# Pacing the up projections of the latent heads between attention steps

## The chip, the cores and the metric

The kernel runs on one core of a Trainium2 chip. The metric is the device time of one execution in microseconds (us). Engines are named as in the profile: PE is TensorE's matmul, PEld its weight load, DVE is VectorE, ACT is ScalarE, POOL is GpSimd, SP is SyncE, which issues the DMAs.

## The reference

One layer of a hybrid encoder, 1024 tokens of width 1024, batch 1, all in float32:

```
mod = silu(c) @ w_ada + b_ada          # 6 rows: shift, scale, gate, twice
h   = rmsnorm(x) * (1 + sc_a) + sh_a
q_lat(256), kv_lat(128), k_rope(32), ca_qkv(3*512) = split(h @ w_in)
q   = rmsnorm(q_lat) @ w_q_up          # 8 heads of 96 = 64 + 32 rotary
kv  = rmsnorm(kv_lat) @ w_kv_up        # 8 heads of 64 (key) + 64 (value)
k   = concat(k_nope, k_rope for every head)
q, k = rope(rmsnorm(q)), rope(rmsnorm(k))
o_mla = softmax(q k^T, chunk-causal, chunks of 64) v
o_ca  = softmax(cq ck^T + rel_bias, band of 9 chunks) cv     # 8 heads of 64
x = x + g_a * (concat(o_mla, o_ca) @ w_out)
h = rmsnorm(x) * (1 + sc_m) + sh_m
gate, val = split(causal_dwconv(h @ w_up, width 3))
x = x + g_m * ((silu(gate) * val) @ w_down)
```

## The kernel before

Every float32 product is made of three matmuls of split operands (high by high, high by low, low by high): `gemm3` writes them, lines 153 to 155 in the profile. The tokens are cut into 8 tiles of 128. The program has three parts: a start (normalising, the first q and k columns), an attention part (from about 86 to 706 us of the profile), and the output projection with the MLP.

**Units of attention.** The attention part goes through 32 units: a head and one half (512) of the queries. First come 16 of chunk attention, named here c, pair, head of the pair, half: c00_0, c00_1, c01_0 up to c31_1. Then 16 of latent attention: m, group of four heads, head, half: m00_0 to m13_1. A unit has scores for its row maxima (`guard`), a step that turns the maxima into a row (`mrow`), and for each block of 128 keys a step of transposed scores with exponentials (`st`) and a step of values (`val`). A unit's blocks are interleaved with the preparation of the unit two ahead (`prep`: turning q and k) and the guards of the unit one ahead. The last `val` of a unit normalises the output and stores it to DRAM (line 846, from tile `ric` for chunk heads and `rim` for latent ones).

**Fillers.** Between attention steps stand pieces of the projections that later units need. They are Python generators in a fixed list: `v0`, `qk1`, `qk2`, `v1`, `qk3` (columns of chunk heads), `m` (the latents: `f_m`), `up0`, `up1` (up projections of the two groups of latent heads), `oca` (the output projection's part over the chunk heads, stored as partial sums). Each `next` on a generator lays a few matmuls of one PSUM tile, with the eviction and the work behind it when the tile is complete, and yields a cost in nanoseconds by a formula of matmul columns alone:

```
yield 3 * len(part) * max(107, w / 2.4 + 2.5)
```

An up projection has two such steps for each token tile: `qu` (six matmuls of 384 columns), whose output is copied (`uqr`, line 616), squared, summed, rooted on POOL (line 119), scaled and rotated on POOL (lines 530 to 533); and `ku` (three matmuls of 512 columns), whose output is copied (`kraw`, line 632), split into values (lines 455 and 457), squared, summed, rooted on POOL and scaled (lines 639 to 644). Its cost counts none of the work after the matmuls.

**The pacing.** `pace` adds the attention step's cost (again from matmul columns) times a ratio to a debt, and lays fillers until their yielded costs have paid it. The ratio is `R_CA` in chunk units and `R_MLA` in latent units. When a unit's preparation needs a filler that is not done, `need` lays the rest of it at once: the latent units need `up0` or `up1`. `fill_step` also calls a side generator, `f_ada`, once for every 2000 of filler cost of `qk1` to `m` (not of `v0`, `up0`, `up1`, `oca`); it loads conditioning weights (`aw`, line 489) and sums them on DVE (`aacc`, lines 491 and 493).

**What sets the order.** The program order so made is a priority. The scheduler of the language then places instructions on each engine's queue, attention steps with a higher priority (`OFF_S`, `OFF_V`), and a filler's matmuls no earlier than an attention matmul four places back (`LAG`). [...]

Of the kernel before, what the change touches and what calls it, by code (L numbers as in the profile page):

```python
# [40 lines left out]
TB = 1  # L41
HI_ON, HL_BUFS = "pa", 3
VSCALE = 2.0 ** 14
R_CA, R_MLA = 1.17, 0.42


C_C, C_GA, C_GM, C_B, C_GQL, C_GKL = 0, 8, 16, 24, 72, 74
# [14 lines left out]
def layer_kernel(ctx, tc, I, out):  # L62
# [9 lines left out]
    def hi_of(eng, o, i):  # L72
        if eng == "a":
            act.activation(o, i, AF.Copy)  # L74
        elif eng == "p":
            pool.tensor_scalar(o, i, 1.0, 0.0, op0=MUL, op1=ADD)  # L76
        else:
            dve.tensor_copy(o, i)

    def lo_of(eng, o, i, hi):  # L80
        (pool if eng == "p" else dve).tensor_tensor(o, i, f32(hi), op=SUB)  # L81
# [34 lines left out]
    def rsqrt_mean(r, ss, n, cols=None):  # L116
        sc = ss if cols is None else ss[:, cols]
        pool.tensor_scalar(sc, sc, 1.0 / n, EPS, op0=MUL, op1=ADD)
        pool.tensor_tensor(r, ss, nhalf[:].to_broadcast(list(r.shape)), op=ALU.pow)
# [17 lines left out]
    def rtile(name, shape=(P, 512), dt=F32):  # L137
        return apg.tile(list(shape), dt, name=name, tag="R", bufs=4)

    def qtile(name):  # L140
        return apg.tile([P, 512], F32, name=name, tag="sq", bufs=2)
# [19 lines left out]
    def gemm3_f(pt, pairs, step=GSTEP):  # L161
        n, w = len(pairs), pt.shape[-1]
        for i0 in range(0, n, step):
            part = pairs[i0:i0 + step]
            if len(trail) > LAG:
                with tc.issue_after(trail[-1 - LAG]):
                    gemm3(pt, part, i0 == 0, i0 + step >= n)
            else:
                gemm3(pt, part, i0 == 0, i0 + step >= n)
            yield 3 * len(part) * max(107, w / 2.4 + 2.5)  # L170
# [218 lines left out]
    def pow2_scale(nm, ssw, b2, n, fac):  # L389
        t = cst.tile([P, 3, ND], F32, name=f"vs{nm}")  # L390
        dve.tensor_tensor(t[:, 0, :n], ssw, b2, op=MUL)
        pt = ps.tile([P, 512], F32, name=f"vsp{nm}", tag="mm", bufs=2)
        pe.matmul(pt[:, :n], ones[:], t[:, 0, :n], start=True, stop=True)
        dve.tensor_reduce(t[:, 1, 0:1], pt[:, :n], axis=AX.X, op=ADD)
        dve.tensor_scalar(t[:, 1, 0:1], t[:, 1, 0:1], fac, 1e-30, op0=MUL, op1=ADD)
        pool.tensor_tensor(t[:, 1, 1:2], t[:, 1, 0:1], nhalf[:], op=ALU.pow)
        ab = cst.tile([P, 2], F32, name=f"vab{nm}")
        dve.tensor_scalar(t[:, 2, 0:1].bitcast(I32), t[:, 1, 1:2].bitcast(I32), 0x7F800000, None, op0=ALU.bitwise_and)
        dve.reciprocal(t[:, 2, 1:2], t[:, 2, 0:1])
        dve.tensor_scalar(t[:, 2, 1:2], t[:, 2, 1:2], 1.0001, None, op0=MUL)  # L400
        dve.tensor_scalar(t[:, 2, 1:2].bitcast(I32), t[:, 2, 1:2].bitcast(I32), 0x7F800000, None, op0=ALU.bitwise_and)
        dve.tensor_scalar(ab[:, 0:1], t[:, 2, 0:1], VSCALE, None, op0=MUL)
        dve.tensor_scalar(ab[:, 1:2], t[:, 2, 1:2], 1.0 / VSCALE, None, op0=MUL)
        return ab[:, 0:1], ab[:, 1:2]
# [42 lines left out]
    def v_tile(pl, name, tag, bufs):  # L447
        v = pl.tile([P, 4, 2, 3, 64], F16, name=name, tag=tag, bufs=bufs)
        pool.memset(v[:, :, 0, 1], 1.0)
        pool.memset(v[:, :, 1, 1], 0.0)  # L450
        return v
# [120 lines left out]
    def g4(shape, dt, name):  # L572
        return G["4"].tile(shape, dt, name=name, tag="G4", bufs=8)

    def g3(shape, dt, name):
        return G["3"].tile(shape, dt, name=name, tag="G3", bufs=16)

    mq, mk, mv = {}, {}, {}

    def f_up(gr):  # L580
        if gr == 0:
            right.__exit__(None, None, None)
            for i in "4v3":
                G["cm" + i] = tc.tile_pool(name="gp" + i, bufs=1, side="right", reuse_waits="tile")
                G[i] = G["cm" + i].__enter__()
        wq = []
        for k in range(2):
            raw = qtile(f"wqr{gr}_{k}")
            sp.dma_start(raw[:, :384], I["w_qu"][gr][:, k, :])
            w = g4([P, 2, 512], F32R, f"wq{gr}_{k}")  # L590
            hi_of("a", w[:, 0, :384], raw[:, :384])
            lo_of("p", w[:, 1, :384], raw[:, :384], w[:, 0, :384])
            wq.append(w)
        raw = qtile(f"wkr{gr}")
        sp.dma_start(raw[:], I["w_kvu"][gr])
        ssw = cst.tile([P, 1], F32, name=f"sswm{gr}")
        junk = qtile(f"wkj{gr}")
        act.activation(junk[:, 0:256].rearrange("p (a b) -> p a b", a=4),
                       raw[:].rearrange("p (a b) -> p a b", a=4)[:, :, NOPE:], AF.Square, accum_out=ssw[:])
        vscale["m", gr] = pow2_scale(f"m{gr}", ssw[:], gb2[:], 1, float(KVR))  # L600
        sc = vscale["m", gr][0]
        wk = g4([P, 2, 512], F32R, f"wk{gr}")
        hi_of("a", wk[:, 0], raw[:])
        lo_of("p", wk[:, 1], raw[:], wk[:, 0])
        for t in range(NT):
            h, j = divmod(t, 4)
            sl = slice(j * P, (j + 1) * P)
            if t % 2 == 0:
                mq[gr, t // 2] = g3([P, 2, 4, QK], F32, f"qn{gr}_{t}")
                mk[gr, t // 2] = g3([P, 2, 4, QK], F32, f"kn{gr}_{t}")  # L610
                mv[gr, t // 2] = v_tile(G["v"], f"vt{gr}_{t}", "Gv", 8)
            pt = ps.tile([P, 512], F32, name=f"qu{gr}_{t}", tag="mm", bufs=2)
            yield from gemm3_f(pt[:, :384], [(latT[k, h][:, 0, sl], latT[k, h][:, 1, sl], wq[k][:, 0, :384], wq[k][:, 1, :384])
                                for k in range(2)])
            raw = rtile(f"uqr{gr}_{t}")
            act.activation(raw[:, :384], pt[:, :384], AF.Copy)
            sq = qtile(f"usq{gr}_{t}")
            act.activation(sq[:, :384], raw[:, :384], AF.Square)
            ss = cst.tile([P, 4], F32, name=f"uss{gr}_{t}", tag="ss", bufs=4)
            r = cst.tile([P, 4], F32, name=f"ur{gr}_{t}", tag="rr", bufs=4)  # L620
            dve.tensor_reduce(ss[:], sq[:, :384].rearrange("p (a b) -> p a b", a=4), axis=AX.X, op=ADD)
            rsqrt_mean(r[:], ss[:], QK)
            q_t = mq[gr, t // 2][:, t % 2]
            dve.tensor_tensor(q_t, raw[:, :384].rearrange("p (a b) -> p a b", a=4),
                              r[:].unsqueeze(2).to_broadcast([P, 4, QK]), op=MUL)
            rope_apply(q_t[:, :, NOPE:], q_t[:, :, NOPE:], tabq, t, 4, raw[:, 0:256])
            pt = ps.tile([P, 512], F32, name=f"ku{gr}_{t}", tag="mm", bufs=2)
            yield from gemm3_f(pt[:], [(latT[2, h][:, 0, sl], latT[2, h][:, 1, sl], wk[:, 0], wk[:, 1])])
            p4 = pt[:].rearrange("p (a b) -> p a b", a=4)
            raw = rtile(f"kraw{gr}_{t}")  # L630
            r3 = raw[:, :256].rearrange("p (a b) -> p a b", a=4)
            act.activation(r3, p4[:, :, 0:NOPE], AF.Copy)
            v_set(mv[gr, t // 2], slice(2 * (t % 2), 2 * (t % 2) + 2),
                  p4[:, :, NOPE:].rearrange("p (c o) b -> p c o b", c=2), sc)
            s3 = raw[:, 256:512].rearrange("p (a b) -> p a b", a=4)
            act.activation(s3, r3, AF.Square)
            ss = cst.tile([P, 4], F32, name=f"kss{gr}_{t}", tag="ss", bufs=4)
            r = cst.tile([P, 4], F32, name=f"kr{gr}_{t}", tag="rr", bufs=4)
            dve.tensor_reduce(ss[:], s3, axis=AX.X, op=ADD)
            pool.tensor_tensor(ss[:], ss[:], ssr[:, t:t + 1].to_broadcast([P, 4]), op=ADD)  # L640
            rsqrt_mean(r[:], ss[:], QK)
            k_t = mk[gr, t // 2][:, t % 2]
            dve.tensor_tensor(k_t[:, :, 0:NOPE], r3, r[:].unsqueeze(2).to_broadcast([P, 4, NOPE]), op=MUL)
            pool.tensor_tensor(k_t[:, :, NOPE:], kr[:, t:t + 1, :].to_broadcast([P, 4, ROPE]),
                               r[:].unsqueeze(2).to_broadcast([P, 4, ROPE]), op=MUL)


    def load_wo(k0, n, he, le):
        ws = []
# [436 lines left out]
    def mt(tag, shape, name, dt=F32):  # L1086
        return mp.tile(list(shape), dt, name=name, tag=tag, bufs=MB[tag])
# [85 lines left out]
    for h in range(2):  # L1173
# [4 lines left out]
        for j in range(NF):  # L1178
# [4 lines left out]
            gr = mt("s", [P, 512], f"gr{h}_{j}")  # L1183
# [10 lines left out]
        for t in range(4):  # L1194
            xt = mt("u", [P, D], f"xo{h}{t}")
            sp.dma_start(xt[:], x1_d[4 * h + t])
            for n in range(2):
                c = slice(n * 512, (n + 1) * 512)
# [78 lines left out]
```

## Time and profile before

| | us |
|---|---|
| median of 3 runs | 1513.79 (1511.94 to 1515.04) |
| the profiled execution | 1509.98 |
| its span in the profile, first to last instruction | 1508.2 |
| PE busy in the span | 1326.6 (88%) |
| DVE busy | 1017.8 (67%) |
| POOL busy | 828.9 (55%) |
| ACT busy | 713.8 (47%) |
| granted clock of TensorE, mean | 0.941 |

Views of the profile are named in words: the page has the share of each engine in 40 slices, in tenths; the table by stage gives each engine's busy time in stretches that one chooses; groups are instructions of one line, engine and operation, with count, busy time and mean duration; waits say which line waited for which; the stores at line 846 tell when each unit of attention ended.

### The profile page before, as it was taken

What the parts mean: (1) busy time and instruction counts of PE and PEld (TensorE: products, weight loads), DVE (VectorE), ACT (ScalarE), POOL (GpSimd) and SP (SyncE); (2) the same over time, 40 slices, a digit from 0 to 9 for tenths busy, and PEclk for the clock granted to TensorE, in tenths of its full rate; (3) what the DMA queues carried; (4) which work ended last, traced back from release to release, by engine and by line L of the source; (5) the groups of instructions that cost most, each with busy time, mean ns of one, the idle gap of its engine ahead of it and who ended that gap; (6) DMA issues with size and microseconds to landing.
All of it is one profiled execution on the core that took longest, in us unless ns stands there. A gap on an engine that the chain in (4) does not pass through costs nothing.

```text
span 1508.2 us, 19999 instructions
## 1 busy us (share of the span) xinstructions
PE 1326.6 (88%) x6926; PEld 1057.8 (70%) x6926; DVE 1017.8 (67%) x1421; ACT 713.8 (47%) x1319; POOL 828.9 (55%) x901
## 2 busy tenths in 40 slices
PE   3769999899878899988927859999999999999997
PEld 2668878778645566655816648888888887887885
DVE  8926676656467756674676668888777788666653
ACT  5435566466446667674354324444444433333331
POOL 5764443363599834222867246666556564665663
PEclk9979999999768899998958979999999999999999
DMA  8321223321110232124621142222222235446442
GB/s 309 122 67 43 71 60 94 93 74 46 57 28 12 65 94 91 58 76 144 216 98 56 56 154 84 84 84 84 72 82 84 85 120 174 146 143 239 156 141 98
DMA packets 80002, 153.02 MB, mean 101 GB/s; under 512 B 8215, under 2 KB 44315, under 8 KB 79901
## 3 DMA queue, kind: packets, MB, share of 16 engines
q1 hardware_dynamic: 79900, 151.75, 30.4%
q8 instruction: 54, 0.88, 0.2%
q14 instruction: 48, 0.39, 0.1%
HBM read 122.88 MB, written 28.84 MB: 101 GB/s over the span
## 4 chain that ended last, share of the span: by engine, by line
PE 49%; DVE 17%; DMA 14%; POOL 10%; issue 6%; ACT 4%; SPq 0%; DVEq 0%; ACTq 0%; POOLq 0%
DMA aw<-w_ada 7%; PE p L1121 5%; PE p L1119 5%; PE p L1120 5%; PE dnp L1193 4%; PE dnp L1191 4%; PE dnp L1192 4%; DMA wu<-w_up 2%; PE tm L810 2%; DVE aacc L493 2%; DVE u L1127 2%; DVE adaw L368 1%; DVE u L1128 1%; PE tc L810 1%; DVE wu L1149 1%
## 5 line engine op out<-in xcount | busy, mean ns | idle before, releaser
L81 POOL TENSOR_TENSOR wds<-wd,wds 128x512 fp32r<-128x512 f32 x88 | 154.2, 1771 | 99.3 <-ACT wds L74 99.2
L74 ACT ACTIVATE wds<-wd 128x512 fp32r<-128x512 f32 x88 | 54.6, 624 | 151.9 <-PE dnp L1193 149.9
L1191 PE MATMUL dnp<-wds,g 128*128 128x512 f32 x308 | 119.6, 390 | 3.8 <-DVE c L1153 1.9
L1193 PE MATMUL dnp<-wds,g 128*128 128x512 f32 x308 | 118.3, 389 | 1.6 <-DVE g L81 1.6
L1192 PE MATMUL dnp<-wds,g 128*128 128x512 f32 x308 | 119.7, 389 | 0.0
L1181 DVE TENSOR_TENSOR wd<-wd,gmbc 128x1024 f32<-128x1024 f32 x44 | 68.0, 1544 | 73.7 <-DMA wd<-w_down 73.7
L81 POOL TENSOR_TENSOR wa<-wu,wa 128x512 fp32r<-128x512 f32 x22 | 38.5, 1749 | 90.7 <-ACT wa L74 90.7
L81 POOL TENSOR_TENSOR wc<-ws,wc 128x512 fp32r<-128x512 f32 x22 | 51.8, 2353 | 65.9 <-ACT wc L74 65.9
L493 DVE SCALAR_TENSOR_TENSOR aacc<-aw,cs,aacc 128x256 f32<-128x256 f32 x84 | 43.4, 517 | 64.5 <-DMA aw<-w_ada 64.0
L821 DVE TENSOR_TENSOR hlm<-pm,hlm 128x512 f16<-128x512 f32 (+2 forms) x96 | 57.6, 608 | 38.4 <-POOL hlm L76 19.6
L81 DVE TENSOR_TENSOR g<-gr,g 128x512 fp32r<-128x512 f32 x44 | 71.0, 1615 | 12.3 <-ACT g L74 12.1
L814 ACT ACTIVATE pc<-tc,sca 128x512 f32<-128x512 f32 (+3 forms) x96 | 50.1, 525 | 60.0 <-DVE hlc L821 45.0
L1127 DVE SCALAR_TENSOR_TENSOR u<-c,pk,u 128x1023 f32<-128x1023 f32 x44 | 75.6, 1726 | 4.1 <-ACT u L1126 4.1
L810 PE MATMUL tm<-qt,kt 96*128 96x512 f16 (+7 forms) x288 | 71.3, 339 | 4.8 <-ACT hlm L818 1.8
L810 PEld LDWEIGHTS <-kt 128*128 128x128 f16 (+2 forms) x480 | 46.1, 101 | 36.5 <-issue 18.4
L1191 PEld LDWEIGHTS dnp<-wds,g 128*128 128x128 f32 x308 | 57.8, 188 | 17.0 <-DVE xo L1199 2.7
L76 POOL TENSOR_SCALAR hlm<-pm 128x384 f16<-128x384 f32 (+2 forms) x48 | 25.7, 535 | 79.4 <-ACT pm L814 50.5
L1126 ACT ACTIVATE u<-c,pk 128x1024 f32<-128x1024 f32 x44 | 52.3, 1236 | 33.8 <-DVE c L1159 33.8
L1193 PEld LDWEIGHTS dnp<-wds,g 128*128 128x128 f32 x308 | 57.8, 188 | 14.2 <-DVE g L81 2.0
L821 DVE TENSOR_TENSOR hlc<-pc,hlc 128x512 f16<-128x512 f32 (+3 forms) x96 | 54.8, 578 | 17.5 <-POOL hlc L76 10.0
L1192 PEld LDWEIGHTS dnp<-wds,g 128*128 128x128 f32 x308 | 57.8, 188 | 11.7
L1128 DVE SCALAR_TENSOR_TENSOR u<-c,pk,u 128x1022 f32<-128x1022 f32 x44 | 65.8, 1530 | 0.0
(432 smaller groups left out, 4714.7 us busy)
## 6 DMA issues: line engine op xcount, KB each, us to landing
wu<-w_up SPq DMA_DIRECT2D x44, 512.0 KB, 3.7
wd<-w_down SPq DMA_DIRECT2D x44, 512.0 KB, 3.5
aw<-w_ada SPq DMA_DIRECT2D x96, 128.0 KB, 2.1
g_d<-u SPq DMA_DIRECT2D x22, 512.0 KB, 2.6
gr<-g_d SPq DMA_DIRECT2D x44, 256.0 KB, 3.1
x<-x SPq DMA_DIRECT2D x16, 512.0 KB, 7.6
adaw<-w_ada_a SPq DMA_DIRECT2D x16, 512.0 KB, 5.0
wq_r<-w_qk SPq DMA_DIRECT2D x32, 128.0 KB, 2.7
```

Of the source, the lines that this page charges most:

```text
L81: (pool if eng == "p" else dve).tensor_tensor(o, i, f32(hi), op=SUB)
L493: dve.scalar_tensor_tensor(acc[:], w[:], cs[:, k:k + 1], acc[:], op0=MUL, op1=ADD)
L810: last = pe.matmul(s[:, c0:c1], l, m, start=(y == 0), stop=(y == len(todo) - 1))
L821: dve.tensor_tensor(hl[:, 1, :w], p[:, :w], hl[:, 0, :w], op=SUB)
L1119: pe.matmul(pt, sh, pg[:, 0], start=(k == 0), stop=False)
L1120: pe.matmul(pt, sh, pg[:, 1], start=False, stop=False)
L1121: pe.matmul(pt, sl, pg[:, 0], start=False, stop=(k == 3))
L1127: dve.scalar_tensor_tensor(u[:, 1:], c[:, :S - 1], pk[:, cv + 1:cv + 2], u[:, 1:], op0=MUL, op1=ADD)
L1128: dve.scalar_tensor_tensor(u[:, 2:], c[:, :S - 2], pk[:, cv:cv + 1], u[:, 2:], op0=MUL, op1=ADD)
L1191: pe.matmul(pts[t][n], sh, w[n][:, 0], start=(j == 0), stop=False)
L1192: pe.matmul(pts[t][n], sh, w[n][:, 1], start=False, stop=False)
L1193: pe.matmul(pts[t][n], sl, w[n][:, 0], start=False, stop=(j == NF - 1))
```

## The change

The generator `f_up` is renamed `f_up_steps`, and a new `f_up` passes its steps on with their costs multiplied by `UP_W` = 4.0. `R_CA` goes from 1.17 to 1.42 and `R_MLA` from 0.42 to 0.64. The list of fillers, their instructions and their tiles are the same; which fillers lie after which attention step is not.

```
-R_CA, R_MLA = 1.17, 0.42
+R_CA, R_MLA = 1.42, 0.64
+UP_W = 4.0
...
-    def f_up(gr):
+    def f_up_steps(gr):
         if gr == 0:
             right.__exit__(None, None, None)
...
+    def f_up(gr):
+        for c in f_up_steps(gr):
+            yield c * UP_W
+
     def load_wo(k0, n, he, le):
```

## The prediction

> **What bounds the kernel now.** I read the page first, for where TensorE is not full. Its slices are 37.7 us each.
>
> ```profile
> span 1508.2 us, 19999 instructions
> PE   3769999899878899988927859999999999999997
> POOL 5764443363599834222867246666556564665663
> PEclk9979999999768899998958979999999999999999
> ```
>
> Counted from slice 0, PE falls to 8, 7, 8, 8 in slices 10 to 13 (377 to 528 us) and is back at 9 after them. In the same four slices POOL stands at 5, 9, 9, 8 and the granted clock at 7, 6, 8, 8. So the kernel has one sick stretch inside its attention part. The other one, slice 20, is the turn to the MLP, which the change does not touch.
>
> Next, the times at which a unit's output is stored (start, duration, queue, line), one row for each unit of attention; they put the stretch into the program. I use these eight; chunk attention writes through `ric`, latent attention through `rim`.
>
> ```profile
> 199.51 0.45 SPq L846 DMA_DIRECT2D oT_d<-ric  x1
> ...
> 235.36 0.45 SPq L846 DMA_DIRECT2D oT_d<-ric  x1
> ...
> 404.71 0.45 SPq L846 DMA_DIRECT2D oT_d<-ric  x1
> 415.64 0.45 SPq L846 DMA_DIRECT2D oT_d<-ric  x1
> 469.65 0.45 SPq L846 DMA_DIRECT2D oT_d<-ric  x1
> ...
> 529.46 0.45 SPq L846 DMA_DIRECT2D oT_d<-rim  x1
> ...
> 666.02 26.64 SPq L846 DMA_DIRECT2D oT_d<-rim  x4
> 706.23 0.45 SPq L846 DMA_DIRECT2D oT_d<-rim  x1
> ```
>
> In order they are the ends of units c01_1, c10_1, c30_1, c31_0, c31_1, m01_0, m11_1 (the first of its four) and m13_1, the last. The table by stage, cut at these ends (us, then busy of PE, PEld, DVE, ACT, POOL with instruction counts, clock, DMA share, GB/s):
>
> ```profile
> 369.00:404.70 35.70, 32.10 (x174) 26.85 (x173) 14.27 (x30) 16.57 (x52) 22.46 (x61) 0.83 0.17 52
> 404.70:529.50 124.80, 99.77 (x443) 67.12 (x443) 85.80 (x198) 71.63 (x157) 102.51 (x189) 0.79 0.13 40
> 415.60:469.60 54.00, 40.57 (x159) 27.11 (x157) 35.35 (x87) 28.67 (x67) 49.31 (x101) 0.72 0.08 22
> 469.60:489.60 20.00, 16.09 (x78) 11.47 (x79) 16.00 (x38) 12.42 (x29) 19.09 (x36) 0.83 0.04 8
> 529.50:666.00 136.50, 126.57 (x728) 82.87 (x727) 86.93 (x167) 97.31 (x178) 43.73 (x50) 1.00 0.26 83
> 666.00:706.20 40.20, 33.26 (x174) 18.03 (x173) 24.11 (x46) 24.67 (x44) 5.56 (x12) 0.88 0.18 52
> ```
>
> From 415.6 to 469.6 POOL is busy 49.31 of 54.0 us (91%) and PE 40.57 (75%) at clock 0.72; from 529.5 to 666 PE is busy 126.57 of 136.5 us (93%) at clock 1.00. What POOL does there, by groups (count | busy, mean ns of one | idle before), and who waits in 400 to 520 us (us in all, times, longest):
>
> ```profile
> L119 POOL TENSOR_TENSOR ur<-uss,nhalf 128x4 f32<-128x4 f32 x16 | 17.5, 1091 | 0.2
> L119 POOL TENSOR_TENSOR kr<-kss,nhalf 128x4 f32<-128x4 f32 x15 | 15.7, 1045 | 0.7
> ACT uqr L616 <- DVE kn L643: 8.6, 4, 2.8
> PE ku L153 <- DVE vt L457: 5.6, 4, 3.0
> ```
>
> These are steps of the up projections: two roots of about 1.05 us for every token tile, hardly any idle time in front of them. TensorE waits at `ku` because the evicting engines are behind. When the sixteen tiles began and ended, and TensorE's part of one tile:
>
> ```profile
> 408.17 0.67 PE L153 MATMUL qu<-wq,latT 128*128 128x384 f32 x1
> 472.87 0.42 PE L153 MATMUL qu<-wq,latT 128*128 128x384 f32 x1
> ...
> 474.47 0.39 PE L155 MATMUL ku<-wk,latT 128*128 128x512 f32 x1
> 515.33 1.01 POOL L119 TENSOR_TENSOR kr<-kss,nhalf 128x4 f32<-128x4 f32 x1
> ```
>
> Sixteen tiles take 515.33 + 1.01 - 408.17 = 108.2 us, 6.8 us each. TensorE needs for one tile's nine matmuls from 472.87 to the last start at 474.47 and one more pitch, about 1.8 us. The lump is paced by POOL and by the chain through it, not by TensorE.
>
> **What the change moves.** No instruction is added or taken away; the order in which fillers are laid between attention steps changes, and the two head groups' tiles with it. By the code's own costs a tile of the up projections counts 975 + 647.5 = 1622.5; now it counts 6490. A pair of chunk units counts 16,404, a pair of latent units 17,870. Before: 16,404 x 1.17 / 1622.5 = 11.8 tiles in a chunk pair. After: 16,404 x 1.42 / 6490 = 3.6, and in a latent pair 17,870 x 0.64 / 6490 = 1.8. Stepping through the pacing with these costs gives: before, `m` ends in c30_0 and all 16 tiles follow in c30_0 to c31_1; the output partials (`oca`, 32 steps) run from m00_0 to m11_1. After, `m` ends in c21_0; 12 tiles come in c21_0 to c31_1 (two of them forced at the preparation of m00_0, which needs the first group), 4 in m00_0 to m02_0, and the 32 steps from m02_1 to m12_0.
>
> **Prices.** (1) A chunk pair: c10 took 235.36 - 199.51 = 35.85 us with 30 filler steps of six matmuls. Their pitch is shown by eleven matmuls in a row, of which the first and the last are:
>
> ```profile
> 205.78 0.28 PE L154 MATMUL ipq<-wq_s,hT 128*128 128x256 f32 x1
> ...
> 206.97 0.28 PE L155 MATMUL ipq<-wq_s,hT 128*128 128x256 f32 x1
> ```
>
> 1.19 us over ten pitches, 0.714 us a step; 35.85 - 21.4 = 14.4 us for 16,404 units of cost, 0.88 us per thousand. (2) A latent unit: 666.0 to 706.2 holds m12 and m13 without fillers, 32,959 of cost in 40.2 us, 1.22 us per thousand. All latent units, 140,019, are 170.8 us. (3) A step of the partials: of 64 matmuls of each kind 529.5 to 666 shows
>
> ```profile
> L154 PE MATMUL oc<-wo,ch 128*128 128x512 f32 x55 | 22.9, 417 | 0.0
> ```
>
> 55, so 27.5 of 32 steps; the units there (m01_1 to m11_1, 82,614) cost 100.8 us, and (136.5 - 100.8) / 27.5 = 1.30 us a step, 41.6 us in all. Partials thus cost the same wherever they lie, and packing them denser is booked at nothing: PE covers them at 93% in that window; were that cover gone, the 7% idle there on 41.6 us is 3 us.
>
> **The sum.** The end of `m` moves ahead of c21_1 and c30: 26,237 x 0.88 = 23.1 us. It also loses its drain. In 369.0 to 404.7 TensorE does 32.10 x 0.83 = 26.6 us of work at full clock, so 9.1 us are lost while the last tiles of `m` are normalised, turned round and followed at once by the up projections, with nothing else to lay between. After the change chunk attention from c21_1 to c31_1 is there to lay between. `m` ends at 404.7 - 23.1 - 9.1 = 372.5 us.
>
> From there to the end of c31_1: by PE alone 42,201 x 0.88 + 12 x 1.8 = 58.7 us; at the lump's pitch 12 x 6.8 = 81.6 us. I take the second: 3.6 tiles a pair is still denser than POOL's 91% row permits at 14.4 us a pair. End: 454.1 (431.2 by the other). Units m00_0 to m02_0: 42,316 x 1.22 + 4 x 1.8 = 58.8 us, POOL far from full; 512.9 (490.0). The rest: 170.8 - 51.6 + 41.6 = 160.8 us; 673.7 (650.8). Before it was 706.2. The gain is 32.5 us (55.4), and what follows, the output projection and the MLP, is unchanged. The profiled execution took 1509.98 us, 3.8 under the median of 1513.79; so 1477.5 there, 1481 for the median (1458 by the other end).
>
> The denser first part: 16,404 x 1.42 in place of x 1.17 lays 35.6 for 29.3 steps of 655 into a chunk pair. That only brings TensorE work forward. Its one other queue is the conditioning's: one filler cost of 2000 calls the next part of it, so those transfers come closer together. Their issues go through SP and their sums through DVE, which waits for them from 86 to 400 us:
>
> ```profile
> DVE aacc L493 <- DMA aw<-w_ada: 59.0, 49, 3.2
> ```
>
> 59.0 us over 49 waits, 1.2 us each, with all attention's DVE work queued behind. PE was full there all the same (c10 above), so I book nothing; if the cover fails, a fifth more waits in the same time is 59.0 x 0.21 = 12 us. A gain there has no ground, as nothing is left out.
>
> **A rule that speaks against it.** In the rows above clock follows feeding: 1.00 at 93% busy, 0.88 at 83% (666 to 706), 0.72 at 75%. [...] What lower rates would make of the time is worked out in the first two rivals.
>
> **Rivals.** Work from 372.5 us to the end of m02_0, at full clock: 37.1 (chunk) + 28.8 (tiles) + 51.6 x 0.83 x 0.88 = 37.7 (latent), 103.6 us. The forecast gives it 140.4 us, a rate of 0.74, as in 666 to 706 (0.83 x 0.88 = 0.73).
> - *Half relief* (0.20): the rate is that of 469.6 to 489.6, 16.09/20.0 x 0.83 = 0.67. 155 us, the end at 688, gain 18: 1496 us. For it: the chain of a tile through four engines is as long as before. Against: there POOL was 95% busy, and it will not be in the latent units.
> - *Spread stall, slower* (0.13): each tile blocks TensorE's queue at `ku` as it does now, and the low clock goes with it over all nine units, at the rate of 415.6 to 469.6: 0.75 x 0.72 = 0.54. 192 us, the end at 725, 19 us later: 1532 us. It turns from gain to loss at 706.2 - 160.8 - 372.5 = 172.9 us, a rate of 0.60. For it: four waits of TensorE at `ku`, and attention's own POOL steps stand in the same queue. Against: 54 us with one POOL-bound lump is what makes 0.54, and the lump is what the weight breaks up.
> - *No spread* (0.04): the scheduler places instructions by its own idea of time; already now tiles written among c30's steps run only after 408. If the 16 stay one lump of 108 us, only its place changes: 1514 us, within 0.2%.
>
> **How the numbers follow.** The forecast has 0.61, with both ends of the one chosen price (1458 to 1481); 0.02 lies below. A measurement of this kernel can tell 0.2%, 3 us, from no change. Faster: 0.61 + 0.02 + 0.20 = 0.83; same 0.04; slower 0.13. The range reaches from a little under the PE-only end, 1455, to 1510, past half relief and up to the same; outside are 0.02, 0.04 and 0.13.
>
> **What would show it.** Right: `qu` starts near 365 to 375 us, spread over more than 130 us; no stretch of 50 us with POOL over 90%; clock from 377 to 528 us above 0.85 and PE over 85%; the last `rim` store near 674. Wrong: a window with POOL at 90% and clock under 0.8 that merely sits 30 us earlier; or PE at 75% and clock 0.8 from c30 through m02; or the DVE's waits for `aw` growing past 70 us.

## The result and the profile after

The changed kernel takes 1510.09 us (median of 20 runs), the kernel before 1512.76 us (20 runs on the same chips); the ratio is 0.998, with a 95% interval of 0.9972 to 0.9989. That is a gain of 2.7 us where 32 were forecast. The profiled execution has a span of 1505.2 us against 1508.2.

The page's slices of the changed kernel, as for the kernel before:

```profile
span 1505.2 us, 19968 instructions
PE   3769999898868899988928759999999999999997
POOL 5764444353698443322867245555556554665662
PEclk9979999999977999999958979999999999999999
```

The sick stretch is still there. POOL has 6, 9, 8, 4 in slices 10 to 13 where it had 5, 9, 9, 8; PE shows 8, 6, 8, 8 there for 8, 7, 8, 8, and a new 8 in slice 9 (339 to 376 us). The unit stores (start, duration, queue, line; the two changed lines and the new function move line 846 to 851):

```profile
398.59 0.45 SPq L851 DMA_DIRECT2D oT_d<-ric  x1
413.50 0.45 SPq L851 DMA_DIRECT2D oT_d<-ric  x1
421.19 0.45 SPq L851 DMA_DIRECT2D oT_d<-ric  x1
469.66 0.45 SPq L851 DMA_DIRECT2D oT_d<-ric  x1
...
548.78 0.45 SPq L851 DMA_DIRECT2D oT_d<-rim  x1
...
704.20 0.45 SPq L851 DMA_DIRECT2D oT_d<-rim  x1
```

These are c30_0, c30_1, c31_0, c31_1, m02_0 and m13_1. c31_1 ends at 469.66, as before (469.65). The turned latents and the up projections, by tile, first and last start at the end of each row, before and after:

```profile
L561 PE MATMUL lt_ps<-ident,lat x24: 270/273/477, 354.3 to 404.1; 128*128 128x128 f32 x24
L155 PE MATMUL qu<-wq,latT x32: 331/338/525, 409.0 to 496.8; 128*128 128x384 f32 x32
```

```profile
L156 PE MATMUL mp<-wm_h,hT x64: 345/353/538, 306.4 to 383.4; 128*128 128x416 f32 x64
L562 PE MATMUL lt_ps<-ident,lat x24: 270/273/477, 339.5 to 401.6; 128*128 128x128 f32 x24
L156 PE MATMUL qu<-wq,latT x32: 331/338/522, 405.5 to 523.3; 128*128 128x384 f32 x32
```

So `m` ends at 401.6 us instead of 404.1, not at 372.5, and the tiles stretch from 405.5 to 523.3 instead of 409.0 to 496.8. The table by stage says what that was worth (us, then busy of PE, PEld, DVE, ACT, POOL, clock last but two); before, then after:

```profile
86.00:386.00 300.00, 282.05 (x2080) 248.48 (x2080) 179.24 (x375) 169.35 (x389) 137.51 (x238) 0.98 0.23 69
386.00:540.00 154.00, 125.37 (x565) 85.22 (x565) 100.61 (x228) 90.06 (x198) 120.91 (x228) 0.79 0.16 48
```

```profile
86.00:386.00 300.00, 277.70 (x2023) 243.64 (x2023) 171.83 (x362) 161.93 (x376) 137.85 (x250) 0.97 0.24 69
386.00:540.00 154.00, 125.73 (x646) 82.87 (x645) 115.87 (x262) 102.35 (x219) 112.29 (x214) 0.86 0.12 35
```

PE busy times clock is taken for TensorE's work at full clock, an estimate: in the kernel before, `qu` matmuls start 0.32 us apart at clock 0.50 (416.36 to 417.00 us) and 0.17 to 0.18 us apart at 0.99 (415.75 to 416.10 us). The clock is given to 0.01, so the first product is good to about 1.4 us. By it the work up to 386 us falls from 276.4 to 269.4 us, and from 386 to 540 us it rises from 99.0 to 108.1. The change loses 7 us in the first stretch and wins 9 in the second. Which of its edits does either is taken apart by two runs below; it is not that the denser laying loses and the thinned tiles win.

### The profile page after: what moved, and what is told of

It is laid out like the page before. It is cut to its first block, busy times and chain, and to the rows that moved or that the text cites. A ratio compares the mean times of both kernels' runs of the same rounds, so it can differ in the third digit from the quotient of the medians.

```text
span 1505.2 us, 19968 instructions
## 1 busy us (share of the span) xinstructions
PE 1323.0 (88%) x6926; PEld 1054.2 (70%) x6926; DVE 1011.6 (67%) x1421; ACT 715.4 (48%) x1319; POOL 818.5 (54%) x901
## 3 DMA queue, kind: packets, MB, share of 16 engines
q1 hardware_dynamic: 79900, 151.75, 30.5%
## 4 chain that ended last, share of the span: by engine, by line
PE 34%; DVE 18%; POOL 16%; DMA 16%; issue 10%; ACT 5%; DVEq 0%; SPq 0%; POOLq 0%; ACTq 0%
DMA aw<-w_ada 7%; POOL wds L82 4%; DMA wu<-w_up 4%; PE tm L815 3%; DVE u L1132 3%; PE dnp L1196 2%; PE dnp L1197 2%; PE dnp L1198 2%; PE p L1126 2%; PE p L1124 2%; PE p L1125 2%; DVE aacc L494 2%; DVE wu L1154 2%; DVE u L1133 2%; DVE adaw L369 1%
## 5 line engine op out<-in xcount | busy, mean ns | idle before, releaser
L82 POOL TENSOR_TENSOR wc<-ws,wc 128x512 fp32r<-128x512 f32 x22 | 55.4, 2520 | 74.2 <-ACT wc L75 74.2
L826 DVE TENSOR_TENSOR hlm<-pm,hlm 128x512 f16<-128x512 f32 (+1 forms) x96 | 58.3, 615 | 32.6 <-POOL hlm L77 17.8
L819 ACT ACTIVATE pm<-tm,scm 128x512 f32<-128x512 f32 (+1 forms) x96 | 55.3, 579 | 27.2 <-PE tm L815 20.6
```

The costliest lines, as they stand in the source:

```text
L819: act.activation(p[:, :w], s[:, :w], AF.Exp, scale=ninv)
L826: dve.tensor_tensor(hl[:, 1, :w], p[:, :w], hl[:, 0, :w], op=SUB)
```

## The experiments

All ratios are to the kernel before in the same sessions. Medians of different rows can come from different sessions, so rows are compared by their ratios; a thousandth is 1.5 us. In the names, `one` leaves seven of eight conditioning loads out, `a5` has five buffers for those loads, `norope` leaves a rotation out, `late` lays the first latent preparations later, `mix` puts output partials between the tiles, `r5` has five R buffers and `dve` moves the rotation to DVE.

| kernel | median us | ratio | 95% interval |
|---|---|---|---|
| changed kernel | 1510.09 | 0.998 | 0.9972 to 0.9989 |
| before_one / after_one | 1494.16 / 1489.09 | 0.9884 / 0.9843 | 0.9868-0.9899 / 0.9828-0.9859 |
| before_a5 / after_a5 | 1502.24 / 1491.52 | 0.9931 / 0.9858 | 0.9916-0.9947 / 0.984-0.9875 |
| rca_only / rca_old | 1506.02 / 1511.96 | 0.9972 / 1.0004 | 0.9951-0.9992 / 0.999-1.0018 |
| before_norope / after_norope | 1491.28 / 1495.89 | 0.9869 / 0.9889 | 0.985-0.9888 / 0.9872-0.9906 |
| before_late / after_late | 1507.03 / 1513.37 | 0.9965 / 0.9995 | 0.9949-0.9981 / 0.998-1.001 |
| rca_a5 / after_late_a5 | 1496.72 / 1504.11 | 0.9882 / 0.9933 | 0.9864-0.9901 / 0.9909-0.9956 |
| after_mix / after_mix_a5 | 1511.22 / 1494.81 | 0.9968 / 0.9871 | 0.9956-0.998 / 0.9849-0.9892 |
| after_late_mix_a5 / before_r5 | 1499.52 / 1515.29 | 0.9889 / 0.9995 | 0.9864-0.9914 / 0.998-1.001 |
| before_a5_dve / after_a5_dve | 1491.95 / 1494.28 | 0.9851 / 0.9854 | 0.9834-0.9867 / 0.9833-0.9876 |

**The fill part: do the conditioning's loads hold `m` back?** Four rows of TensorE and DVE from 344 to 349 us of the changed kernel (start, duration, instruction, idle time in front and what ended it):

```profile
344.10 0.37 PE L763 MATMUL sc<-bg,identr 128*128 128x256 f32 x1
...
347.35 0.48 DVE L494 SCALAR_TENSOR_TENSOR aacc<-aw,cs,aacc 128x256 f32<-128x256 f32 x1 [2.07 <-DMA aw<-w_ada]
347.75 0.42 DVE L771 TENSOR_REDUCE mz<-sc 128x1 f32<-128x256 f32 x1
348.22 0.32 PE L755 MATMUL sc<-kt,qt 128*128 128x384 f16 x1 [2.39 <-DVE mz L771]
```

The last matmul of the scores `sc` ends at 344.47. DVE stands 2.07 us for one load, the row maximum of those scores starts behind the load's sum, at 347.75, and TensorE stands 2.39 us for that maximum. The waits from 86 to 400 us before and after, and in the changed kernel with five buffers:

```profile
DVE aacc L493 <- DMA aw<-w_ada: 59.0, 49, 3.2
```

```profile
DVE aacc L494 <- DMA aw<-w_ada: 61.5, 48, 3.4
```

```profile
DVE aacc L494 <- DMA aw<-w_ada: 32.3, 34, 2.4
```

The first two edits leave seven of eight loads out, the other two give the tiles more buffers:

```
-                    w = atile(f"aw{m}_{n}_{k}")
-                    sp.dma_start(w[:], I["w_ada"][k * P:(k + 1) * P, c0:c0 + 256])
+                    if k == 0:
+                        w = atile(f"aw{m}_{n}_{k}")
+                        sp.dma_start(w[:], I["w_ada"][k * P:(k + 1) * P, c0:c0 + 256])
...
-        return apg.tile([P, 256], F32, name=name, tag="A", bufs=3)
+        return apg.tile([P, 256], F32, name=name, tag="A", bufs=5)
```

> The changed kernel with the conditioning sums f_ada reading one weight tile for each group of eight (the other seven loads are left out, so shift, scale and gate of two rows come out other than in the reference; DVE still does all its sums). Theory A (the chain of aw loads, with DVE waiting in its queue for each, sets when m ends): the last turned latent lt_ps leaves from 402 us to 375-385, the first qu comes before 390, DVE's waits for aw between 128 and 405 fall from 61.5 us to under 15, and the whole time falls by 20 to 35 us against before. Rival B (m's own chain through ACT and POOL and the R buffers sets its end): lt_ps ends at 395-402, gain 0 to 8 us. Rival C (TensorE is simply full up to 400, denser fillers only displace attention): lt_ps ends a little earlier, attention later, gain 0 to 8 us.

> The kernel before with the same seven of eight aw loads left out. Theory A: the waits for aw go here too (59.0 us to under 15) and m ends earlier by what the chain cost, but the lump of up projections still follows: gain 5 to 20 us, at least 10 us less than the changed kernel gains by the same edit. Rivals B and C: within 5 us of before.

> The changed kernel with 5 instead of 3 buffers for f_ada's tiles (tag A), nothing left out. Theory A: three or four aw loads are in flight instead of one or two, DVE's waits for aw fall from 61.5 us to 10-35, lt_ps ends 8 to 25 us earlier and the time falls by 8 to 25 us below the changed kernel's. Rivals B and C: within 4 us of the changed kernel.

> The kernel before with 5 instead of 3 buffers for tag A, nothing left out. Theory A: waits for aw fall, gain 3 to 15 us, less than in the changed kernel. Rivals B and C: within 4 us of before.

Without the loads both kernels win: 21.0 us with the change (1510.1 to 1489.1), 17.7 without it (1511.8 to 1494.2). With five buffers it is 18.6 and 9.6 us. So the loads cost both kernels a real stall, and rivals B and C fall as explanations of that. Theory A asked for more: the kernel before was to gain at least 10 us less than the changed one from leaving the loads out, and it gains only 3 less. The last `lt_ps` leaves after_one at

```profile
L563 PE MATMUL lt_ps<-ident,lat x24: 270/272/329, 329.9 to 385.7; 128*128 128x128 f32 x24
```

385.7, at the edge of the expected 375 to 385, but before_one, without the denser laying, has it at 389.6. The last `lt_ps` with five buffers, before and after:

```profile
L561 PE MATMUL lt_ps<-ident,lat x24: 272/273/448, 351.5 to 403.8; 128*128 128x128 f32 x24
```

```profile
L562 PE MATMUL lt_ps<-ident,lat x24: 270/273/476, 331.7 to 393.7; 128*128 128x128 f32 x24
```

Here the change moves `m`'s end by 10.1 us, not 2.5, and it is worth 11 us (0.9931 to 0.9858). So the loads did hold back a part of the gain; without them it is 6 us (0.9884 to 0.9843), and in no pair the 32 us forecast.

**The laid order and the queue's order.** In TensorE's instruction stream one can count how many of the 192 blocks of transposed scores have begun before a filler. A pair of chunk units has 12 blocks: c21_0 begins at 60, c30_0 at 72, c31_1 at 88, m00_0 at 96.

```
              m's last matmul    the 16 tiles of the up projections, each at block
laid, before        72-75        all from 72 to 95
laid, after         60-63        1 to c21_0, 12 by block 95, 4 in m00_0 to m02_0 (96 to 123)
before                83         90 x8 | 96 x3, 98, 100 x2, 103, 105
after                 75         86, 89, 90 x6 | 95, 96 x2, 98, 100, 108, 112, 122
rca_only              72         78, 82, 84, 86, 90 x4 | 96 x3, 98, 100 x2, 102, 104
rca_old               88         90 x8 | 96 x4, 104, 108, 117, 124
before_late           82         93, 94, 96 x6 | 100 x6, 103, 106
after_late            75         86, 88, 90, 92, 94, 96 x3 | 98, 100 x2, 102, 108, 115, 120, 129
```

The scheduler runs attention, with its higher priority, ahead of fillers up to the point where attention needs them: block 90, where the preparation of m00_1 needs the whole first group. In the changed kernel six of its eight tiles still stand in that one place; only the last four, laid in latent units, stand about where they were laid. The lump is still there in the table by stage of the changed kernel, at the same place, with POOL at 91% and the clock at 0.72:

```profile
421.00:470.00 49.00, 38.08 (x151) 25.80 (x152) 31.46 (x79) 27.03 (x61) 44.78 (x90) 0.72 0.08 21
```

The roots of `ur` on POOL up to 470 us, in the kernel before, then in the changed one:

```profile
L119 POOL TENSOR_TENSOR ur<-uss,nhalf 128x4 f32<-128x4 f32 x9 | 9.1, 1011 | 0.2
```

```profile
L120 POOL TENSOR_TENSOR ur<-uss,nhalf 128x4 f32<-128x4 f32 x10 | 10.3, 1031 | 0.1
```

Nine tiles against ten are through this root by the end of c31_1, where 16 and 12 were laid (TensorE had begun `qu` of eleven and twelve). Two kernels take the change apart, `R_CA` alone (`R_CA, R_MLA = 1.42, 0.42`, no weight) and the rest alone (`1.17, 0.64`, weight 4):

> The kernel before with R_CA = 1.42 alone: the denser laying of fillers in the chunk units, no weight. Theory S (the chip does not follow the laid order: attention runs at higher priority and fillers go where TensorE is free, so m's end on the chip hangs on the work in front of it and not on the unit it is laid in): the last lt_ps stays within 5 us of 404, although the ratio lays it two units earlier; units c20_0 to c30_0 end 15 to 30 us later than before; the whole is 0 to 10 us slower than before. Rival P (the prediction's accounting: m's end moves with the attention laid behind it): lt_ps ends at 370-380, the lump of sixteen tiles follows from there, and the whole is 5 to 12 us faster (the drain of m is covered).

> The changed kernel with R_CA back at 1.17: weight 4 and R_MLA 0.64 alone, the part up to m's end laid as before (12 up steps are then forced at once at the preparation of m00_0). Theory S with two parts of opposite sign (the fill part of the changed kernel loses some 9 us of TensorE work up to 386 us, the up part wins some 8): lt_ps ends at 402-406 as before, and the whole is 4 to 10 us faster than before. Rival P: without the earlier m the tiles cannot be spread, the forced steps make a lump again, and the whole is within 3 us of before.

The weight and `R_MLA` alone give nothing (1.0004); `R_CA` alone gives as much as the whole change (0.9972). That is neither expectation: theory S had the two parts the other way round, with rca_only 0 to 10 us slower, and it was 5.8 us faster; rca_old was to win 4 to 10 us and did not. The last `lt_ps` of rca_only starts at

```profile
L561 PE MATMUL lt_ps<-ident,lat x24: 271/273/477, 338.5 to 396.6; 128*128 128x128 f32 x24
```

396.6: neither within 5 us of 404, as S wanted, nor at 370 to 380, as the prediction's accounting (rival P) wanted, but nearer to S. The table by stage, rca_only first, then rca_old:

```profile
86.00:386.00 300.00, 276.25 (x1998) 242.47 (x1996) 170.78 (x356) 159.31 (x375) 139.57 (x257) 0.96 0.25 72
386.00:540.00 154.00, 123.74 (x689) 85.08 (x688) 114.13 (x254) 102.54 (x218) 118.90 (x211) 0.96 0.14 42
```

```profile
86.00:386.00 300.00, 282.65 (x2077) 246.66 (x2075) 182.11 (x378) 169.35 (x386) 136.55 (x233) 0.98 0.24 69
386.00:540.00 154.00, 118.66 (x584) 81.17 (x584) 104.50 (x239) 92.80 (x206) 113.25 (x224) 0.85 0.11 31
```

By the same product as above `R_CA` alone loses 11.2 us of TensorE's work up to 386 us (265.2 for 276.4) and wins 19.8 from 386 to 540 us (118.8 for 99.0), with no tile weighted. The weight and `R_MLA` alone have 277.0 and 100.9, both within 2 us of the kernel before. So both the loss and the win come with the denser laying, not with the weight. That attention pushed behind 386 us is there to cover the lump is a reading that fits; no run isolates it.

**Is the lump paced by POOL?** One line goes from `f_up`: `rope_apply(q_t[:, :, NOPE:], ...)`.

> The kernel before without the rotation of q in the up projections (four POOL instructions for each token tile left out, 8.7 + 8.4 + 6.2 + 6.1 = 29.4 us of POOL in all; q is then not rotated). If the lump is paced by POOL: the sixteen tiles take 108.2 - 29 = about 80 to 88 us, and the whole is 15 to 28 us faster. If it is paced by TensorE's own work or by the chain of a tile: under 8 us faster.

> The changed kernel with the same rotation left out. If the weight has taken POOL out of the way: under 8 us faster than the changed kernel. If POOL still paces the tiles up to c31_1's end (10 of 16 tiles lie there): 8 to 18 us faster, less than the kernel before wins by the same cut.

The kernel before wins 20.5 us of the 29.4 taken from POOL, the changed one 14.2 (1510.09 to 1495.89), as both were expected to if POOL paces the tiles. In the kernel before, from first to last `qu`:

```profile
L155 PE MATMUL qu<-wq,latT x32: 333/338/522, 405.8 to 473.1; 128*128 128x384 f32 x32
```

67.3 us, where it was 87.8. POOL paces the lump, as the prediction read the 91%. With POOL relieved the change has no lead left: 0.9869 without it, 0.9889 with it, in intervals that overlap.

**If the tiles do stand apart.** The preparation of the first two latent units goes one unit later:

```
-        if n + 2 < U:
-            tasks.append(lambda v=units[n + 2]: ready(v))
+        for i in ((n + 1, n + 2) if n == 16 else (n + 1,) if n == 15 else () if n == 14 else (n + 2,)):
+            if i < U:
+                tasks.append(lambda v=units[i]: ready(v))
```

> The changed kernel with the preparation of the first two latent units laid one unit later (m00_0 in c31_1, m00_1 in m00_0). In TensorE's instruction order of the changed kernel six of the first group's eight tiles stand in one place, behind block 90 of 192 (third block of c31_1), where attention stops because the next preparation needs the whole group; here the tiles stand at blocks 86, 88, 90, 92, 94, 96, 96, 96, 98, 100, 100, 102, 108, 115, 120, 129. Theory L (what the weight was to do, it does not do as laid: attention runs ahead of the fillers to the point where it needs the group, and the lump stays there): now the weight works, c31_1 ends by 455 instead of 470, and the whole is 6 to 20 us faster than the changed kernel. Rival T (a tile costs its POOL and chain time wherever it stands, spread or not): within 4 us of the changed kernel.

> The kernel before with the same later preparation. Its tiles stand at blocks 93, 94, six at 96, six at 100, 103, 106: two lumps again, only behind the end of c31_1. Theory L: no gain, within 4 us of before. Rival T: the same. A gain over 6 us would say that the later preparation helps by itself and not through the spread.

Theory L falls, as far as it says that the lost spread was the lost gain. The tiles do stand apart now, and c31_1 ends at 443.5 us (426.06 + 17.46, the second of the row's two), 26 us sooner; but by m02_0 (543.86 for 548.78) 5 us are left of that, and the whole is at 0.9995, and before_late, with its two lumps, at 0.9965, 5 us faster, a little over the 4 us that both theories allowed. Where the 26 us went:

```profile
426.06 17.46 SPq L851 DMA_DIRECT2D oT_d<-ric  x2
...
543.86 0.45 SPq L851 DMA_DIRECT2D oT_d<-rim  x1
```

```profile
443.00:510.00 67.00, 48.14 (x226) 31.48 (x225) 48.04 (x112) 36.29 (x78) 47.08 (x89) 0.75 0.06 15
```

From 443 to 510 us, m00_0 and m00_1, TensorE is busy 72% at clock 0.75, a rate of 0.54, with POOL at 70% only. Its waits in 440 to 560 us, here and in the changed kernel:

```profile
PE sm L755 <- DVE mz L771: 12.6, 12, 2.7
```

```profile
PE sm L755 <- DVE mz L771: 2.4, 4, 0.8
```

The guards' chain (scores, row maximum on DVE, next scores through one PSUM buffer) lies open. One reason could be that the partials stand behind `up1` in the list, so that thin tiles keep them out; the next runs try it.

**Partials between the tiles, and the other buffers.** `fill_step` takes every second filler from the partials while `up1` is at the head of the list (a `flip[0]` toggled for `key == "up1" and ca_done`, then `key, gen = fillers[1]`).

> The changed kernel with fillers of the output partials laid in turn with those of up1 once latent values have begun: partials then stand from block 100 to 163 of TensorE's order in place of 124 to 167; nothing else moves. Theory M (the weighted tiles stand in the place of the partials, and the latent units m00 to m02 starve): units m00_1 to m02_0 end 8 to 15 us earlier, the whole is 5 to 15 us faster than the changed kernel. Rival R (every tile holds TensorE back through its evictions, R buffers and POOL, wherever it stands and whatever stands beside it): within 4 us of the changed kernel, the latent units later win it back no better.

> The same with five buffers for f_ada's tiles. Theory M: 5 to 12 us faster than the changed kernel with five buffers alone, that is 1480 to 1487 us. Rival R: 1488 to 1496.

> The same with the later preparation of the first two latent units as well, so that the tiles stand apart and have partials between them. Theory M: the loss of the later preparation with five buffers (1504.1 against 1491.5 us) was starvation of m00 and m01, and most of it comes back: 1482 to 1494 us. Rival R: 1500 or more.

> Both together: the changed kernel with five buffers for f_ada's tiles and the later preparation of the first two latent units. If the two losses are separate and theory L holds, 6 to 16 us faster than with the buffers alone: 1475 to 1486 us. Rival T: 1488 to 1495.

after_mix is at 0.9968 against 0.998, the intervals overlap, and m02_0 ends at 547.6 us instead of 548.8, where 8 to 15 us were expected; after_mix_a5 is at 0.9871 against 0.9858, no gain. after_late_a5 missed both expectations: 0.9933, 11 us slower than the buffers alone. In the version whose tiles stand apart partials bring back 7 us by the ratios (0.9933 to 0.9889), with intervals that overlap by 0.0005. The wait that they were to cover is hardly shorter: from 430 to 560 us TensorE waits 8.9 us in `sm` for `mz` in after_late_mix_a5, where partials begin at block 100, and 11.1 us in after_late_a5, where they begin at block 132. So missing partials are not shown to be what opens the guards' chain, and at most a small part of it. The rival that every tile holds TensorE back through the R buffers got an experiment of its own (tag R with five buffers):

> The kernel before with five instead of four R buffers (the copies uqr and kraw that a tile's evictions write). Theory R: TensorE's waits for ACT uqr and DVE vt in 404 to 530 us fall, the lump shortens by 5 to 15 us, and the whole is 4 to 12 us faster than before. Otherwise (POOL's own 85 us pace the lump): within 4 us.

0.9995: in the kernel before the fifth buffer does nothing, and its R buffers do not pace the lump. In the thinned order the R buffers were not tried.

**Rotation on DVE.** `rope_apply` takes the engine as an argument and `f_up` hands it `dve`; tag A has five buffers.

> The kernel before with the same two edits. If POOL's time paces the lump: 8 to 18 us faster than with the buffers alone (1502.2), 1484 to 1494 us, so that the changed order's lead of some 11 us shrinks to under 8. If DVE is as tight: within 4 us of 1502.2.

> The changed kernel with five buffers for f_ada's tiles and the rotation of q in the up projections on DVE instead of POOL (29.4 us of POOL's time moved). If POOL's time is what a tile costs, also in the thinned order: 6 to 14 us faster than with the buffers alone, 1478 to 1486 us. If DVE, with attention's work in its queue, is as tight as POOL: within 4 us of 1491.5, or slower.

The kernel before goes from 0.9931 to 0.9851, the changed one stays (0.9858 and 0.9854). In the kernel before, moving this work off POOL pays. In the changed one it does not, although leaving the same work out won 14.2 us there (with three buffers): the two runs do not tell a POOL that no longer paces from a DVE that is as tight. With both stalls eased the change is worth nothing: 1491.95 without it, 1494.28 with it.

**R_CA with five buffers.**

> The kernel before with R_CA = 1.42 and five buffers for f_ada's tiles: the changed kernel's first part without weight and without R_MLA, the conditioning's waits eased. Theory L: its first group's tiles stand at 78, 80, 82, 85 and four at 90 (with weight six at 90), so it is as fast as the changed kernel with five buffers (1491.5 us) or up to 6 us faster: the gain of the change is that of R_CA. Rival T2 (weight and R_MLA give the gain once the conditioning is out of the way): 4 to 9 us slower than 1491.5.

0.9882 against 0.9858 of after_a5: 4 us slower by the ratios, with intervals that overlap by 0.001. Its last `lt_ps` starts at 384.3 us, 19.5 us earlier than in before_a5. Whether weight and `R_MLA` add something once the loads are eased stays open. Of all versions that leave nothing out, after_a5 (1491.5 us) beats both kernels with the smallest edit, and before_a5_dve does as well without the change.

## Why the prediction was wrong, step by step

*`m` ends at 372.5 us.* This step failed first: 401.6. It booked 23.1 us because c21_1 and c30 are laid behind `m`'s end. The laid order is a priority, and attention runs ahead of it: by 12 blocks `m` was laid earlier, by 8 it stands earlier in TensorE's stream (83 to 75), and by 2.5 us on the chip, since the units in front of it end later (c30_0 at 398.59 instead of about 369). That is not all of it: with five buffers for the loads the same change moves the end by 10.1 us, so the conditioning's waits, which the prediction booked at nothing, hid a part. The 9.1 us of its drain did not go either. POOL's queue at that place in the changed kernel:

```profile
391.00 1.01 POOL L82 TENSOR_TENSOR wq<-wqr,wq 128x384 fp32r<-128x384 f32 x1 [3.47 <-ACT wq L75]
...
393.28 0.72 POOL L120 TENSOR_TENSOR mr<-mss,nhalf 128x2 f32<-128x2 f32 x1
```

The splitting of the up projections' weights stands ahead of the last latent's root, and POOL waits 3.47 us for ACT before it; I had named SP and DVE as the queues to be passed, and not this one. From the last `mp` to the last `lt_ps` pass 18.2 us (383.4 to 401.6), as in the kernel before, where it is 17.5 (386.6 to 404.1).

*Dense filling costs nothing.* In the changed kernel 7 us of TensorE's work are missing up to 386 us; with five buffers it is 1.8 (284.02 x 0.98 against 285.02 x 0.97), no more than the rounding of the clock. Five buffers win 18.6 us with the denser laying and 9.6 without it. The 9 us between are near the term for a lost cover (12 us) that the prediction had worked out and booked at nothing. The sum of DVE's waits grew by 2.5 us only, not by the fifth from which that term was reckoned.

*12 tiles at 6.8 us to the end of c31_1.* 68.1 us (469.7 - 401.6) instead of 81.6. Ten tiles are through `ur` by then, 6.8 us each, so the pitch of the lump held; TensorE had begun twelve. That the term came out so near is in part luck: it was to hold the chunk units from c21_1 on, and c21_1 (385.57) and c30_0 (398.59) had ended before it began.

*m00_0 to m02_0 in 58.8 us.* 79.1 us (548.8 - 469.7), the second failed term, 20 us. TensorE is not slower there than in the tail from which the price was taken, it has more to do. The stage, then the guards' scores in it and in that tail (666.0 to 706.2 us of the kernel before):

```profile
470.00:549.00 79.00, 67.76 (x353) 40.92 (x351) 61.76 (x127) 53.46 (x107) 48.40 (x87) 0.89 0.13 36
```

```profile
L755 PE MATMUL sm<-kt,qt 96*128 96x512 f16 (+3 forms) x33 | 9.7, 348 | 2.4 <-DVE mz L771 2.4
```

```profile
L750 PE MATMUL sm<-kt,qt 96*128 96x512 f16 (+3 forms) x12 | 3.4, 326 | 2.8 <-DVE mz L766 2.8
```

The rate is 67.76 x 0.89 / 79 = 0.76, the forecast's was 0.74. But the stage does 60.3 us of work at full clock where 44.9 were booked (37.7 + 7.2). Guards, their rows and preparations (`sm`, `mrm_ps`, `mq_ps`, `mk_ps`) take 23.3 us of PE for the five units here and 7.2 for the four units that end in the tail, where much of theirs had run before 666 us; the price of 1.22 us per thousand was taken from a stretch that lacked them. Three steps of the partials, 9.0 us of PE, ran here too, and on POOL six tiles were left, not four.

*The rest in 160.8 us.* 155.4 (704.2 - 548.8): three steps of the partials, booked here at 1.30 us each, had run in the stage before, and the price of a step, taken from a window with guards and preparations in it, made up for the price of a unit. The sum of the four differences, 29.1 - 13.5 + 20.3 - 5.4, is the 30.5 us between the forecast end of attention, 673.7, and 704.2.

*The rivals.* "No spread", given 0.04, is what happened to the first group: its lump stayed where attention needs it. It should have had the greatest chance, as my own text held its evidence (tiles laid in c30 that ran only after 408). "Spread stall" described after_late: rate 0.54 in two latent units. What was right is the reading of the lump itself, POOL at 91% and 6.8 us a tile; before_norope and before_a5_dve show that taking POOL's work out of it pays 20 and 12 us (the second against before_a5). That thinner tiles win by themselves did not come: the weight and `R_MLA` alone are at 1.0004. The clock rose as forecast, from 0.79 to 0.86 in 386 to 540 us, but not with TensorE's busy share, which is 81% and 82%; rca_only has 0.96 at 80%, and of the prediction's own rows 369 to 404.7 has 0.83 at 90% and 666 to 706 has 0.88 at 83%. In the lump of the kernel before the clock stays at 0.50 for 16.9 us, though PE waits no longer than 0.8 us at a time there and is busy 78%:

```profile
416.30:433.20 16.90, 13.13 (x34) 9.39 (x34) 10.81 (x27) 6.91 (x18) 15.84 (x35) 0.50 0.12 31
```

That is a lower clock at more feeding than the 0.72 at 75% of the row from 415.6 to 469.6, so "clock follows feeding" does not hold beyond the three rows from which the prediction read it. What holds the clock down in the lump no run isolates.

Still open is why the thinned order costs as much as the lump: the guards' chain lies open there, but partials between the tiles closed little of it. Open too is whether the weight adds anything once the loads are eased.

## What to carry to other kernels

Where a scheduler places instructions by priority, weights in the order of emission reach the queues only as far as something holds the favoured work back: read the order in which the instructions stand on the engine, and from which point the favoured work must wait, before pricing a new spread. The lump that POOL paced got shorter by taking work off POOL (67.3 us from first to last `qu` where it was 87.8); laying it thinner gave nothing here (1.0004). A price taken from the end of a part misses the work that its units had already done ahead. And a wait for a DMA with few buffers cost more here than the engine that waited: DVE stood 2.07 us for one load, and TensorE 2.39 us for the maximum behind it. Two more buffers of 1 KB a partition were worth 10 to 19 us, against 2.7 us of the change.

## What the runs showed of the hardware that I had not expected

A root (`pow`) of a few numbers on POOL is dear for its size: 128x4 took 1.04 and 1.09 us on the mean of sixteen (`kr` and `ur`) in the kernel before and 128x2 took 0.72 us (`mr` above), while the rotation's products of 128x128 took 0.54 and 0.52 us (lines 530 and 531). Two roots of 128x4 make 2 of the 5.3 us of POOL in a tile (84.5 us over sixteen tiles in 409 to 515 us of the kernel before). In the kernel before, moving the rotation's four small instructions a tile, 29.4 us of POOL, to DVE was worth 12 us (0.9931 to 0.9851) although TensorE had waited for DVE in the part before: for the row maximum `mz` alone 9 times, 6.9 us, from 86 to 400 us.
